# A two-layer trunk in split fp32 on one core: other PSUM banks for the short TensorE work, other steps for the seven-product form

## The chip, the cores and the metric

The kernel runs on one core of one Trainium2 chip. The metric is the device time of one execution in microseconds (us). The kernel before took 1900.27 us, the median of three runs (1898.66 to 1901.03). The trace was taken from a further execution, which took 1902.93 us as a whole, while the program's own instructions spanned 1900.6 us of it.

## The reference

The input is 256 tokens of 2048 numbers. Two layers follow one another, each a token mixer and a dense FFN, with an RMS norm ahead of each and a residual add behind it; a last norm ends it. The mixer of layer 0 is a causal pooling, that of layer 1 an attention with eight heads, each the difference of two softmaxes.

```python
def pool_mixer(h, w_grp, scale):            # layer 0; windows 2, 4, 8, 16
    ...
    pooled = jnp.stack([causal_trailing_mean(hg[:, :, g], POOL_WINDOWS[g]) for g in range(N_POOL_GROUPS)], axis=2)
    y = jnp.einsum('bsgc,gcd->bsgd', pooled - hg, w_grp)
    return y.reshape(B, S, D) * scale

def diff_attention(h, w_qkv, ...):          # layer 1
    qkv = h @ w_qkv
    ...
        s = jnp.where((dist >= 0)[None, None, None], s + bias[None, :, None], -jnp.inf)
        p = jax.nn.softmax(s, axis=-1)
        a = p[:, :, 0] - lam * p[:, :, 1]
        return jnp.einsum('bhqk,bkhe->bqhe', a.astype(v.dtype), v)
    ...
    o = rmsnorm(o, subln_g) * (1.0 - lambda_init)
    return o.reshape(B, S, H * e) @ w_o

def swiglu(h, wg, wu, wd):                  # wg, wu: 2048 x 5632, wd: 5632 x 2048
    return (jax.nn.silu(h @ wg) * (h @ wu)) @ wd
```

## The kernel before, in words

**One step of a group.** All large products go through `group` (line 139). A group gives a block of 256 tokens by 1024 columns as four blocks of 128 by 512, one for each half of the tokens and half of the columns. It adds up *steps*; each step takes 256 rows of the contraction, that is one activation tile (`xp`, `xq`, `h` or `oT`) and one weight load of 1 MB (`raw`, line 110). Every fp32 operand is split in a high and a low half: of the weights ScalarE writes the high half (`whi`, line 116) and VectorE the low one (`wlo`, line 117). A product of blocks is then three matmuls (high by high, high by low, low by high).

**Two forms of step.** A *plain* step makes the eight block products of a 2 by 2 multiplication: 24 matmuls. A *seven-product* step makes seven products of sums of blocks: 21 matmuls. For it VectorE adds the weight blocks (`tsum`, lines 122 to 125), ScalarE and VectorE split the sums (`thi` line 131, `tlo` line 132), and the activation tile is stored as eight sums of its blocks (the long branch of `pair`, lines 247 to 255). `tsum`, `thi` and `tlo` have one buffer each, `raw`, `whi` and `wlo` three. Which steps of a group are seven-product is written in the constants of lines 38 to 41.

**Banks.** The eight PSUM banks have fixed roles (line 136). The seven products go to banks 0 to 6 (M1 is 0, M6 1, M7 2, P5 3, P3 4, P4 5, M2 6). A plain step's four sums go to banks 6, 4, 5 and 7, three of which it shares with the seven products M2, P3, P4. So banks 0 to 3 are touched by seven-product steps alone. At the end of a group `combined` (line 182) makes the four blocks from the banks with two ScalarE copies (lines 188, 192) and eight VectorE operations (lines 189 to 198) into four SBUF tiles; a group of plain steps alone needs none of it, and returns the banks themselves.

**Short work.** Transposes (line 237 in `pair`, 441, 488), scores (456), the products with v (505 to 507) and the pooling products (311, 313) take a bank from `aux` (line 80), which goes round through banks 5, 6 and 7. A bank is a tile with one buffer: a later user in program order waits until the earlier one is read out. The pooling stage's sums take banks 0 to 4 through `acc`.

**Order.** The program lists, group by group, the steps, the combination and then the short work on the result. A scheduler of the framework lays down each engine's order when the kernel is built: of what its own reckoning has ready, it takes what comes first in the program, so that TensorE may go on with steps of the next group among short work of this one, unless banks or data forbid it.

**Stages.** Pooling mixer (lines 264 to 345), FFN of layer 0, attention, FFN of layer 1. An FFN goes in three chunks of 4, 4 and 3 groups of gate and up (eight steps each; scaled and multiplied at lines 368 and 369, transposed into `h`), and each chunk is followed by two groups of down (eight steps, six in the last chunk), which are added to the residual `x_tok` (line 387). In the last chunk of layer 0 the new residual is also transposed at once into the operand of the attention (line 396). Attention has four groups for q and k (line 478; scaled at 481, then two heads each), two groups for v (line 498; scaled at 501, then four heads each, which end in `oT`, line 517) and two for the output projection (line 520). The kernel ends with the last norm: squares (line 218), the row factor (lines 222, 207 to 212, 224), the scaling of the output tiles (lines 404 and 406) and four stores (line 407), two from SyncE's queue and two from ScalarE's.

Of the kernel before, what the change touches and what calls it, by code (L numbers as in the profile page):

```python
# [9 lines left out]
F32 = mybir.dt.float32  # L10
# [17 lines left out]

PLAIN = 2
WINDOWS = (2, 4, 8, 16)  # L30
LAMBDA_INIT = 0.8 - 0.6 * math.exp(-0.3)
QK_SCALE = 128.0 ** -0.5
MASKED = 1.0e30
# [1 line left out]
CHUNKS = (4, 4, 3)  # L35


SEVEN = (1, 4, 6)
SEVEN_DOWN = (1, 4)
SEVEN_QKV = (1, 4)  # L40
SEVEN_O = ()


B12, B11, B22, B21 = range(4)
# [6 lines left out]
def trunk_kernel(ctx, tc, x_n, gains, scale_in, final_in, subln, lam_in, band, dist,  # L51
# [21 lines left out]
    def bank(i, shape=(P, 512)):  # L73
        return psum.tile(list(shape), F32, name=f"b{i}", tag=f"b{i}")

    def acc(shape=(P, 512)):
        turn["acc"] += 1
        return bank(turn["acc"] % 5, shape)

    def aux(shape=(P, 512)):  # L80
        turn["aux"] += 1
        return bank(5 + turn["aux"] % 3, shape)


    gain_sb = const.tile([P, 6, NK], F32, name="gain_sb")
# [180 lines left out]
    with tc.tile_pool(name="start", bufs=1, reuse_waits="tile") as st:  # L266

        warm = tmp.tile([P, 8], F32, name="warm", bufs=1)
        nc.scalar.activation(warm[:, 0:1], ones[:, 0:1], AF.Sqrt)
        wp = aux()  # L270
        for _ in range(WARM):
            nc.tensor.matmul(wp[:, 0:P], ones, ones, start=True, stop=True)

        band_sb = st.tile([P, 4, 3, P], F32, name="band_sb")
        for t in range(2):
            for i in range(2):
                cols = slice(i * 1024, (i + 1) * 1024)
                nc.sync.dma_start(out=x_tok[:, t, cols], in_=x_n[:, t, cols])
        nc.scalar.dma_start(out=band_sb, in_=band)
        nc.scalar.dma_start(out=gain_sb, in_=gains)  # L280
        w_plain = [st.tile([P, 4, 512], F32, name=f"w{g}") for g in range(PLAIN)]
        for g in range(PLAIN):
            nc.sync.dma_start(out=w_plain[g], in_=pool_w[g])

        for t in range(2):
            ss_in = tmp.tile([P, 2, 4], F32, name="ss")
            sq = st.tile([P, 1024], F32, name="sq_in", bufs=2)
            for i in range(2):
                nc.scalar.activation(sq, x_tok[:, t, i * 1024:(i + 1) * 1024], AF.Square, accum_out=ss_in[:, 0, i:i + 1])
            tot = tmp.tile([P, 2], F32, name="ss_tot")  # L290
            nc.vector.tensor_tensor(tot[:, 0:1], ss_in[:, 0, 0:1], ss_in[:, 0, 1:2], ALU.add)
            r = rsqrt(tot[:, 0:1], D, 1)
            part = band_sb[:, :, 0:2] if t == 0 else band_sb[:, :, 2:3]
            nc.vector.tensor_scalar(part, part, r, None, ALU.mult)
        scale_sb = st.tile([P, D], F32, name="scale_sb")
        nc.scalar.dma_start(out=scale_sb, in_=scale_in)
        nc.scalar.dma_start(out=dist_sb, in_=dist)
        zp = [None] * 4

        def group_product(g):  # L300

            zp[g] = [acc() for _ in range(2)]
            if g < PLAIN:
                w = w_plain[g]
            else:
                hi, lo = halves(load(pool_w[g]))
            for i in range(2):
                ps = aux((P, 2, S))
                for k in range(2):
                    cols = slice((4 * g + 2 * i + k) * P, (4 * g + 2 * i + k + 1) * P)  # L310
                    nc.tensor.matmul(ps[:, k], x_tok[:, 0, cols], band_sb[:, g, 0:2].rearrange("p b s -> p (b s)"),  # L311
                                     start=True, stop=False)
                    nc.tensor.matmul(ps[:, k, P:], x_tok[:, 1, cols], band_sb[:, g, 2], start=False, stop=True)
                for k in range(2):
                    at = 2 * i + k
                    gain = gain_sb[:, 0, 4 * g + at:4 * g + at + 1]
                    if g < PLAIN:
                        a = st.tile([P, S], F32, name="mean", bufs=4)
                        nc.scalar.activation(a, ps[:, k], AF.Copy, scale=gain)
                        for t in range(2):  # L320
                            nc.tensor.matmul(zp[g][t], a[:, t * P:(t + 1) * P], w[:, at], start=(at == 0), stop=(at == 3))  # L321
                        continue
                    a = st.tile([P, 2, S], F32R, name="mean_hl", bufs=4)
                    split(a, ps[:, k], gain)
                    for t in range(2):
                        ah, al = (a[:, j, t * P:(t + 1) * P] for j in range(2))
                        for j, (u, y) in enumerate(((ah, hi), (ah, lo), (al, hi))):
                            nc.tensor.matmul(zp[g][t], u, y[:, at], start=(at == 0 and j == 0), stop=(at == 3 and j == 2))  # L328

        def residual(g):  # L330
            cols = slice(g * 512, (g + 1) * 512)
            for t in range(2):
                y = st.tile([P, 512], F32, name="y", bufs=2)
                nc.vector.tensor_tensor(y, zp[g][t], scale_sb[:, cols], ALU.mult)
                nc.vector.tensor_tensor(x_tok[:, t, cols], y, x_tok[:, t, cols], ALU.add)
                square_sum(ss, t, g)
            transposed(xq, g, 2, SEVEN)

        group_product(0)
        group_product(1)  # L340
        residual(0)
        group_product(2)
        residual(1)
        group_product(3)
        residual(2)
        residual(3)

    def ffn(layer, xq, ss, next_op, next_gain):
# [3 lines left out]
        with tc.tile_pool(name=f"ffn{layer}", bufs=1, reuse_waits="tile") as hp:  # L352
            g0 = 0
            ys = []
            for c, n in enumerate(CHUNKS):
# [19 lines left out]
                for o in range(2):  # L375
                    if last and o == 1:
# [1 line left out]
                        pre = tmp.tile([P, 8], F32, name="warm", bufs=1)  # L378
                        nc.scalar.activation(pre[:, 0:1], x_tok[:, 0, 0:1], AF.Square)
                        nc.scalar.activation(pre[:, 0:1], pre[:, 0:1], AF.Sqrt)  # L380
                    cs = combined(group([(hp_tiles[i], i in SEVEN_DOWN, w_down[layer][o, 2 * g0 + i])
                                         for i in range(2 * n)], hp), hp)
                    for b in range(2):
                        j = 2 * o + b
# [8 lines left out]
                                nc.vector.tensor_tensor(ys[j][:, t], x_tok[:, t, cols],  # L393
                                                        final_sb[j // 2][:, j % 2 * 512:j % 2 * 512 + 512], ALU.mult)
                        if last and next_op is not None:
                            transposed(next_op, j, next_gain, SEVEN_QKV)
                g0 += n
            if next_op is None:

                r = row_scale(ss_next)  # L400
                for j in range(4):
                    for t in range(2):
                        if t:
                            nc.vector.tensor_scalar(ys[j][:, t], ys[j][:, t], r[:, t:t + 1], None, ALU.mult)
                        else:
                            nc.scalar.activation(ys[j][:, t], ys[j][:, t], AF.Copy, scale=r[:, t:t + 1])
                    (nc.scalar if j % 2 else nc.sync).dma_start(
                        out=out[:, j * 512:(j + 1) * 512].rearrange("(t p) n -> p t n", p=P), in_=ys[j])
        return ss_next

    xp = operand(SEVEN_QKV)
    ss = ffn(0, xq, ss, xp, 3)


    ss_next = tmp.tile([P, 2, 4], F32, name="ss")
    with tc.tile_pool(name="attn", bufs=1, reuse_waits="tile") as ap_, ExitStack() as heads:
        at = heads.enter_context(tc.tile_pool(name="attn_tmp", bufs=2, reuse_waits="tile"))
        small = ap_.tile([P, 64], F32, name="small")
        qs_col, subln_sb, lam_sb, lp, le, neg_lam, gs = (
# [10 lines left out]
        nc.vector.scalar_tensor_tensor(neg_lam, le[:, 1:2], -LAMBDA_INIT, le[:, 0:1], ALU.add, ALU.subtract)  # L430
        nc.vector.tensor_scalar(gs, subln_sb, 1.0 - LAMBDA_INIT, None, ALU.mult)
        aT = []

        def transpose_probs(h, probs):

# [39 lines left out]

        for g in range(4):

            cs = combined(group([(xp[p], p in SEVEN_QKV, w_qk[g, p]) for p in range(NP)], ap_), ap_)
            for t in range(2):
                for b, scale in enumerate((qs_col, r_col)):  # L480
                    nc.scalar.activation(cs[t][b], cs[t][b], AF.Copy, scale=scale[:, t:t + 1])
            for u in range(2):
                qk = at.tile([P, 2, 2, S], F32, name="qk", bufs=3)
                for b in range(2):
# [10 lines left out]

        oT = [None] * NP
        for g in range(2):
            cs = combined(group([(xp[p], p in SEVEN_QKV, w_v[g, p]) for p in range(NP)], ap_), ap_)
            for b in range(2):
                for t in range(2):  # L500
                    nc.scalar.activation(cs[t][b], cs[t][b], AF.Copy, scale=r_col[:, t:t + 1])
            for h in range(4 * g, 4 * g + 4):
                v = [cs[t][h % 4 // 2][:, h % 2 * E:(h % 2 + 1) * E] for t in range(2)]
                op = aux((P, 2, E))
# [8 lines left out]
                on = at.tile([P, 2, E], F32, name="o_n", bufs=1)  # L513
                for t in range(2):
                    nc.scalar.activation(on[:, t, :], op[:, t, :], AF.Copy, scale=ro[:, t:t + 1])
                oT[h] = op_.tile(pair_shape(h in SEVEN_O), F32R, name=f"oT{h}")
                pair(oT[h], lambda i, t: on[:, t, i * P:(i + 1) * P], [gs[:, i:i + 1] for i in range(2)], h in SEVEN_O)
        xq = operand(SEVEN)
        for g in range(2):
            cs = combined(group([(oT[p], p in SEVEN_O, w_o[g, p]) for p in range(NP)], ap_), ap_)  # L520
            for b in range(2):
                j = 2 * g + b
                cols = slice(j * 512, (j + 1) * 512)
# [89 lines left out]
```

## Time and profile before

| | |
|---|---|
| median of three runs | 1900.27 us |
| profiled execution: its time, its span | 1902.93 us, 1900.6 us |
| TensorE busy, matmuls | 1854.4 us, 8248 |
| VectorE busy | 1554.5 us |
| ScalarE busy | 1010.3 us |
| read from HBM | 353.29 MB |
| granted TensorE clock, mean | 0.993 |

Times in the trace count from the span's start. A row of the timeline shows start, duration, engine, line, operation, output and inputs, shape and count, and in brackets the idle time of the engine ahead of it with what ended that. Matmuls overlap: the recorded duration of one is longer than the distance to the next, so that the cost of a matmul in a stream is read from the distance of starts. An fp32 matmul that isn't split appears as two records. PEld is TensorE's load of its stationary operand. PEclk is the share of full speed that TensorE's clock was granted.

The stages as the trace shows them: the pooling mixer to about 62 us, the FFN of layer 0 to 764, q and k to about 975, v and the heads' outputs to about 1095, the output projection to about 1186, the FFN of layer 1 to the end.

### The profile page before, as it was taken

Reading aid. Unit: us, or ns where it says so; the run is one execution under the profiler, and the core shown is the slowest. Engines: PE = TensorE matmul, PEld = TensorE weight load, DVE = VectorE, ACT = ScalarE, POOL = GpSimd, SP = SyncE. Lnnn points to the kernel's source line nnn. Section 1 sums busy time; section 2 is a strip of 40 time slices with the busy share of each in tenths; the row PEclk is TensorE's granted clock in tenths of the full one; section 3 lists DMA queues with packets and bytes.
Section 4 is the critical chain, followed back from the end, with each engine's and each line's share of the span. In section 5 each row is a group of like instructions: output and inputs, shape, how many; then the busy total and the mean of one; then the engine's idle time right before and its main releaser. Section 6 shows DMA issues by size and latency. Waiting matters only on the chain.

```text
span 1900.6 us, 20799 instructions
## 1 busy us (share of the span) xinstructions
PE 1854.4 (98%) x8248; PEld 1510.3 (79%) x8248; DVE 1554.5 (82%) x1577; ACT 1010.3 (53%) x979; POOL 0.7 (0%) x6
## 2 busy tenths in 40 slices
PE   8999999999999999999999999999999999999996
PEld 5788888888888887777777788888888888888885
DVE  4798988889888898977786645888878989888887
ACT  5565554555545556555555544555544555445554
POOL 0000000000000000000000000000000000000000
PEclk9999999999999999999999999999999999999998
DMA  6455565555555555544443545555655555565552
GB/s 263 156 199 200 179 210 209 185 206 200 190 203 189 199 182 197 185 163 152 163 155 133 177 155 180 177 196 189 211 201 207 191 200 196 199 230 189 200 200 89
DMA packets 50720, 356.72 MB, mean 188 GB/s; under 512 B 5952, under 2 KB 6080, under 8 KB 8000
## 3 DMA queue, kind: packets, MB, share of 16 engines
q1 hardware_dynamic: 49216, 351.30, 53.2%
q10 hardware_dynamic: 1408, 4.11, 0.6%
q8 instruction: 64, 1.05, 0.2%
q14 instruction: 32, 0.26, 0.0%
HBM read 353.29 MB, written 2.10 MB: 187 GB/s over the span
## 4 chain that ended last, share of the span: by engine, by line
PE 90%; DVE 5%; ACT 2%; DMA 2%; issue 1%; SPq 0%; ACTq 0%; DVEq 0%
PE b L178 86%; PE b L237 2%; DVE wlo L117 1%; ACT whi L116 1%; DMA raw<-w_qk 1%; DMA raw<-pool_w 1%; PE b L328 1%; PE b L321 1%; DVE x_tok L387 0%; DMA x_tok<-x_n 0%; PE b L456 0%; ACT sq L218 0%; DVE s_sb L458 0%; PE b L311 0%; DVE xp L230 0%
## 5 line engine op out<-in xcount | busy, mean ns | idle before, releaser
L178 PE MATMUL b<-whi,xp 128*128 128x512 f32 x2844 | 916.4, 393 | 5.0 <-DVE oT L230 2.2
L116 ACT CAST whi<-raw 128x2048 fp32r<-128x2048 f32 (+1 forms) x330 | 587.3, 1786 | 616.6 <-PE b L178 465.1
L117 DVE TENSOR_TENSOR wlo<-raw,whi 128x2048 fp32r<-128x2048 f32 (+1 forms) x330 | 700.6, 2129 | 233.2 <-ACT whi L116 231.6
L178 PEld LDWEIGHTS b<-whi,xp 128*128 128x128 f32 x2844 | 534.2, 188 | 123.8 <-issue 5.0
L178 PE MATMUL b<-wlo,xp 128*128 128x512 f32 x1422 | 557.1, 392 | 1.2 <-DVE wlo L117 1.2
L178 PE MATMUL b<-whi,h 128*128 128x512 f32 x1168 | 370.3, 390 | 1.1 <-ACT e L250 1.1
L178 PEld LDWEIGHTS b<-wlo,xp 128*128 128x128 f32 x1422 | 268.0, 188 | 56.3 <-DVE wlo L117 1.9
L178 PEld LDWEIGHTS b<-whi,h 128*128 128x128 f32 x1168 | 218.7, 188 | 47.3 <-ACT e L250 2.1
L132 DVE TENSOR_TENSOR tlo<-tsum,thi 128x2048 fp32r<-128x2048 f32 x98 | 223.9, 2285 | 14.9 <-ACT thi L131 14.3
L178 PE MATMUL b<-wlo,h 128*128 128x512 f32 x584 | 227.5, 390 | 0.2 <-DVE wlo L117 0.2
L178 PE MATMUL b<-thi,xp 128*128 128x512 f32 x592 | 209.6, 394 | 0.0
L131 ACT CAST thi<-tsum 128x2048 fp32r<-128x2048 f32 x98 | 187.2, 1911 | 24.2 <-DVE tsum L125 24.1
L122 DVE TENSOR_TENSOR tsum<-raw 128x1024 f32<-128x1024 f32 x98 | 119.5, 1219 | 15.3 <-DMA raw<-w_down 7.2
L178 PEld LDWEIGHTS b<-thi,xp 128*128 128x128 f32 x592 | 110.6, 188 | 22.4 <-ACT thi L131 0.4
L178 PEld LDWEIGHTS b<-wlo,h 128*128 128x128 f32 x584 | 109.7, 188 | 23.3 <-DVE wlo L117 0.6
L178 PE MATMUL b<-tlo,xp 128*128 128x512 f32 x296 | 115.7, 391 | 0.0
L178 PE MATMUL b<-whi,oT 128*128 128x512 f32 x256 | 82.7, 401 | 2.2 <-DVE oT L230 2.2
L124 DVE TENSOR_TENSOR tsum<-tsum,raw 128x512 f32<-128x512 f32 x98 | 67.5, 689 | 2.4
L125 DVE TENSOR_TENSOR tsum<-tsum,raw 128x512 f32<-128x512 f32 x98 | 67.3, 687 | 2.0
L178 PE MATMUL b<-thi,h 128*128 128x512 f32 x192 | 67.9, 393 | 1.0 <-ACT thi L131 1.0
L178 PEld LDWEIGHTS b<-tlo,xp 128*128 128x128 f32 x296 | 55.6, 188 | 11.8 <-DVE tlo L132 0.6
L178 PEld LDWEIGHTS b<-whi,oT 128*128 128x128 f32 x256 | 49.1, 193 | 12.9 <-issue 2.7
(127 smaller groups left out, 1143.1 us busy)
## 6 DMA issues: line engine op xcount, KB each, us to landing
raw<-w_gu SPq DMA_DIRECT2D x176, 1024.0 KB, 4.8
raw<-w_down SPq DMA_DIRECT2D x88, 1024.0 KB, 4.9
raw<-w_qk SPq DMA_DIRECT2D x32, 1024.0 KB, 5.1
raw<-w_v SPq DMA_DIRECT2D x16, 1024.0 KB, 4.8
raw<-w_o SPq DMA_DIRECT2D x16, 1024.0 KB, 4.9
x_tok<-x_n SPq DMA_DIRECT2D x4, 512.0 KB, 7.2
w<-pool_w SPq DMA_DIRECT2D x2, 1024.0 KB, 12.0
raw<-pool_w SPq DMA_DIRECT2D x2, 1024.0 KB, 13.3
```

Of the source, the lines that this page charges most:

```text
L116: nc.scalar.copy(hi[:, lo_block:], raw[:, lo_block:])
L117: nc.vector.tensor_tensor(lo[:, lo_block:], raw[:, lo_block:], f32(hi[:, lo_block:]), ALU.subtract)
L122: nc.vector.tensor_tensor(t[:, T1:T3 + 1], raw[:, B11:B22 + 1], raw[:, B12:B12 + 1].broadcast_to([P, 2, 512]), ALU.add)
L124: nc.vector.tensor_tensor(t[:, T2], t[:, T1], raw[:, B22], ALU.add)
L125: nc.vector.tensor_tensor(t[:, T4], t[:, T2], raw[:, B21], ALU.add)
L131: nc.scalar.copy(hi, t)
L132: nc.vector.tensor_tensor(lo, t, f32(hi), ALU.subtract)
L178: nc.tensor.matmul(ps[b], x, y[:, block], start=first, stop=(left[b] == 0))
L237: nc.tensor.transpose(ps[:, i, 1 - t if seven else t], src(i, t), ident)
L321: nc.tensor.matmul(zp[g][t], a[:, t * P:(t + 1) * P], w[:, at], start=(at == 0), stop=(at == 3))
L328: nc.tensor.matmul(zp[g][t], u, y[:, at], start=(at == 0 and j == 0), stop=(at == 3 and j == 2))
```

## The change

`aux` goes round through banks 0 to 3, `acc` through banks 4 to 7. The seven-product steps of gate and up move from 1, 4, 6 to 2, 4, 6 (the first group of each layer keeps 6 alone), those of down from 1, 4 to 2, 5, those of q and k from 1, 4 to 4, 6. v has plain steps alone, which are scaled from the banks into SBUF tiles of their own; the very last group of down has plain steps alone too. The sums of q and k get a pool of their own. The scaling of q and k goes column half by column half. In the pooling product the second block of the band, which is zero outside 16 columns, is a matmul of 16 columns of its own in place of the right half of a 256-column one. Of the last scaling, ScalarE keeps two of eight pieces in place of four.

```diff
+HALO = 16
-SEVEN = (1, 4, 6)
-SEVEN_DOWN = (1, 4)
-SEVEN_QKV = (1, 4)
-SEVEN_O = ()
+SEVEN = (2, 4, 6)
+SEVEN_DOWN = (2, 5)
+SEVEN_QK = (4, 6)
...
     def acc(shape=(P, 512)):
         turn["acc"] += 1
-        return bank(turn["acc"] % 5, shape)
+        return bank(4 + turn["acc"] % 4, shape)
 
     def aux(shape=(P, 512)):
         turn["aux"] += 1
-        return bank(5 + turn["aux"] % 3, shape)
+        return bank(turn["aux"] % 4, shape)
...
-                    nc.tensor.matmul(ps[:, k], x_tok[:, 0, cols], band_sb[:, g, 0:2].rearrange("p b s -> p (b s)"),
-                                     start=True, stop=False)
-                    nc.tensor.matmul(ps[:, k, P:], x_tok[:, 1, cols], band_sb[:, g, 2], start=False, stop=True)
+                    nc.tensor.matmul(ps[:, k, 0:P], x_tok[:, 0, cols], band_sb[:, g, 0], start=True, stop=True)
+                    nc.tensor.matmul(ps[:, k, P:], x_tok[:, 1, cols], band_sb[:, g, 2], start=True, stop=False)
+                    nc.tensor.matmul(ps[:, k, P:P + HALO], x_tok[:, 0, cols], band_sb[:, g, 1, 0:HALO], start=False, stop=True)
...
-                    cs = combined(group([(hp_tiles[i], i in SEVEN_DOWN, w_down[layer][o, 2 * g0 + i])
+                    by_seven = () if last and o and next_op is None else SEVEN_DOWN
+                    cs = combined(group([(hp_tiles[i], i in by_seven, w_down[layer][o, 2 * g0 + i])
                                          for i in range(2 * n)], hp), hp)
...
-                            transposed(next_op, j, next_gain, SEVEN_QKV)
+                            transposed(next_op, j, next_gain, SEVEN_QK)
...
-                        if t:
+                        if t or j > 1:
                             nc.vector.tensor_scalar(ys[j][:, t], ys[j][:, t], r[:, t:t + 1], None, ALU.mult)
...
+        hq = heads.enter_context(tc.tile_pool(name="qk_sums", bufs=1, reuse_waits="tile"))
...
+        def scaled(cs, scales, pool=None):
+            out = [[pool.tile([P, 512], F32, name="tok", tag=f"tok{t}{b}", bufs=2) if pool else cs[t][b] for b in range(2)]
+                   for t in range(2)]
+            for b, scale in enumerate(scales):
+                for t in range(2):
+                    nc.scalar.activation(out[t][b], cs[t][b], AF.Copy, scale=scale[:, t:t + 1])
+            return out
...
-            cs = combined(group([(xp[p], p in SEVEN_QKV, w_qk[g, p]) for p in range(NP)], ap_), ap_)
-            for t in range(2):
-                for b, scale in enumerate((qs_col, r_col)):
-                    nc.scalar.activation(cs[t][b], cs[t][b], AF.Copy, scale=scale[:, t:t + 1])
+            cs = combined(group([(xp[p], p in SEVEN_QK, w_qk[g, p]) for p in range(NP)], hq), hq)
+            cs = scaled(cs, (qs_col, r_col))
...
-            cs = combined(group([(xp[p], p in SEVEN_QKV, w_v[g, p]) for p in range(NP)], ap_), ap_)
-            for b in range(2):
-                for t in range(2):
-                    nc.scalar.activation(cs[t][b], cs[t][b], AF.Copy, scale=r_col[:, t:t + 1])
+            cs = scaled(combined(group([(xp[p], False, w_v[g, p]) for p in range(NP)], op_), op_), (r_col, r_col), op_)
```

More of the change, by code (lines that the diff above doesn't have):

```diff
@@ L409, in ffn @@
         return ss_next
-    xp = operand(SEVEN_QKV)
+    xp = operand(SEVEN_QK)
     ss = ffn(0, xq, ss, xp, 3)
@@ L515, in trunk_kernel @@
                     nc.scalar.activation(on[:, t, :], op[:, t, :], AF.Copy, scale=ro[:, t:t + 1])
-                oT[h] = op_.tile(pair_shape(h in SEVEN_O), F32R, name=f"oT{h}")
-                pair(oT[h], lambda i, t: on[:, t, i * P:(i + 1) * P], [gs[:, i:i + 1] for i in range(2)], h in SEVEN_O)
+                oT[h] = op_.tile(pair_shape(False), F32R, name=f"oT{h}")
+                pair(oT[h], lambda i, t: on[:, t, i * P:(i + 1) * P], [gs[:, i:i + 1] for i in range(2)], False)
         xq = operand(SEVEN)
         for g in range(2):
-            cs = combined(group([(oT[p], p in SEVEN_O, w_o[g, p]) for p in range(NP)], ap_), ap_)
+            cs = combined(group([(oT[p], False, w_o[g, p]) for p in range(NP)], ap_), ap_)
             for b in range(2):
```

## The prediction

> **What bounds the kernel now.** I read the page's busy times first, then the timeline of TensorE inside an FFN group, then the windows, one for each kind of group, and last the waits of TensorE.
>
> ```profile
> PE 1854.4 (98%) x8248; PEld 1510.3 (79%) x8248; DVE 1554.5 (82%) x1577; ACT 1010.3 (53%) x979; POOL 0.7 (0%) x6
> ```
>
> TensorE is busy for 98% of the span, but busy isn't at its peak: a matmul that waits behind its predecessor or runs at a lower clock counts as busy. So I need the price of a matmul in an undisturbed stream.
>
> ```profile
> 600.42 0.39 PE L178 MATMUL b<-wlo,xp 128*128 128x512 f32 x1
> 600.64 0.62 PE L178 MATMUL b<-whi,xp 128*128 128x512 f32 x2
> 601.10 0.39 PE L178 MATMUL b<-wlo,xp 128*128 128x512 f32 x1
> ```
>
> Three starts in 0.68 us: 0.2267 us for one matmul of line 178. A plain step is 24 of them (5.44 us), a seven-product step 21 (4.76 us). The pooling stage gives the short ones:
>
> ```profile
> 26.56 0.59 PE L311 MATMUL b<-band_sb,x_tok 128*128 128x256 f32 x2
> 26.99 0.38 PE L313 MATMUL b<-band_sb,x_tok 128*128 128x128 f32 x2
> 27.21 0.60 PE L311 MATMUL b<-band_sb,x_tok 128*128 128x256 f32 x2
> ```
>
> A record of 256 columns takes 0.215 us to the next start (0.43 for two), one of 128 columns 0.11, and a transpose has that last shape. Now the windows: one in the FFN, then one from the first scaling of a q and k group (809.43) to that of three groups later, one from the first scaling of the first v group to that of the second, one from there to the first read of the output projection's sums (1132.10); the last two rows split a stall of this stage from what follows it. Columns: length, busy time and records of PE, PEld, DVE, ACT and POOL, granted clock, DMA share, GB/s.
>
> ```profile
> 142.00:184.00 42.00, 42.00 (x191) 34.79 (x190) 37.12 (x33) 22.48 (x17) 0.00 (x0) 1.00 0.57 195
> 809.43:964.73 155.30, 149.06 (x669) 118.25 (x668) 120.28 (x188) 85.83 (x122) 0.00 (x0) 0.98 0.46 161
> 1015.59:1072.68 57.09, 52.39 (x228) 42.05 (x227) 32.78 (x49) 32.53 (x52) 0.00 (x0) 0.97 0.42 147
> 1072.68:1132.10 59.42, 54.49 (x230) 43.31 (x229) 26.91 (x39) 28.32 (x48) 0.00 (x0) 0.94 0.40 136
> 1086.00:1092.20 6.20, 3.68 (x16) 2.27 (x15) 2.44 (x11) 3.96 (x15) 0.00 (x0) 1.00 0.00 0
> 1092.20:1099.00 6.80, 5.79 (x16) 4.58 (x17) 1.76 (x6) 2.12 (x5) 0.00 (x0) 0.50 0.00 0
> ```
>
> In the FFN TensorE is never idle, so there is nothing to win there but matmuls. In attention there is.
>
> - A q and k group has 186 matmuls (42.2 us), 22 transposes and eight short score records (30 x 0.11 = 3.3) and eight of 256 columns (1.7): 47.2 us. The window gives 155.30 / 3 = 51.8. Lost: 4.6 us a group, 18.4 in four.
> - A v group has 186 matmuls (42.2), 24 records of 256 columns (5.2) and 16 transposes (1.8): 49.2 of 57.09, lost 7.9. The second v group's heads run under the output projection, with 192 matmuls (43.5): 50.5 of 59.42, lost 8.9. Together 16.8.
>
> So 35 of the 1900 us are lost in attention. Who held TensorE:
>
> ```profile
> PE b L178 <- DVE oT L230: 4.4, 2, 2.2
> PE b L237 <- ACT o_n L515: 3.7, 5, 1.0
> PE b L456 <- ACT aT L443: 2.5, 4, 0.6
> PE b L456 <- ACT qk L490: 2.0, 4, 0.7
> PE b L178 <- DVE xp L230: 1.9, 3, 1.0
> PE b L456 <- DVE s_sb L458: 1.5, 4, 0.4
> ```
>
> The first row is the telling one. Matmuls of line 178 do not read `oT` of the head just made; they waited 2.2 us twice for VectorE to read it out of its bank:
>
> ```profile
> 1093.21 0.76 PE L178 MATMUL b<-whi,oT 128*128 128x512 f32 x1 [2.22 <-DVE oT L230]
> ```
>
> This is a plain step of the output projection on early heads. Its data had been there, its bank (5, 6 or 7) had not: `aux` had lent it to the heads. Behind it, TensorE being in order, stood everything else. The scores' waits for `aT` and `s_sb` are waits for a lent bank too; those for `o_n` and `qk` are for data.
>
> **The change part by part.**
>
> *Banks 0 to 3 for the short work.* Plain steps touch banks 4 to 7 alone, so the next group's steps up to its first seven-product one can run whatever the heads are doing. In q and k that is now step 4: 4 x 5.44 = 21.8 us of free matmuls, against heads whose short work ran from its first transpose to its last for 18 us:
>
> ```profile
> 811.43 0.27 PE L488 MATMUL b<-ident,c 128*128 128x128 f32 x1
> ```
> ```profile
> 829.30 0.34 PE L441 MATMUL b<-ident,a_sb 128*128 128x128 f32 x1
> ```
>
> And VectorE then also had a seven-product step 1 to make, which it no longer has there. In v and the output projection no step needs banks 0 to 3 at all. So the bank waits go, and with them the low clock that followed them. What is late next is data: a transpose that the scheduler placed a little ahead of the ScalarE or VectorE result it takes. The two rows of that kind above sum to 5.7 us over all heads; I keep 0.95 us a q and k group and 1.5 us for each four output heads, 6.8 in all. Gain: 18.4 - 3.8 = 14.6 in q and k, 16.8 - 3.0 = 13.8 in v and output. Bounds: 35 (no residual) to 17 (half the loss stays as waits for data).
>
> The clock is part of that gain. In the 6.20 us up to 1092.2 TensorE was busy for 3.68, and in the 6.80 us that follow it was granted 0.50, which cost 3.4 us. By the Trainium skill, TensorE: Matmul & The Clock Gate, section "HAM oscillation", the clock falls back after a gap of over some 3.4 us without TensorE work; the trace disagrees, since the longest wait in the rows above is 2.2 us. By that rule the low clock would have another cause and stay, and the sum would be smaller by the second rival's price.
>
> *v plain.* Four seven-product steps become plain: 12 matmuls, 12 x 0.2267 = +2.7 us, all of it on TensorE's path. What goes is the VectorE work of those steps and the combination, which lay under matmuls.
>
> *Seven-product steps moved.* Same count in the FFN and in q and k, so no matmul is added; the cover is that VectorE has idle time (37.12 of 42 us busy). Price if the cover is gone: see the second rival. In the six-step groups of the last chunks, the last step is now a seven-product one, so that the combination starts late: five VectorE operations behind the last products, 5 x 0.68 = 3.4 us, hold banks 4, 5 and 7 for up to 3 us into the next group. The next plain step reaches its last bank only after 18 matmuls (4.1 us), so I expect under 1 us each time, at three places. Against it stand the waits for `xp` above (1.9 us, at the seam of layer 0's FFN and attention, largely for lent banks), which go. Net -1, bounds -2 and +3.
>
> *Band of 16 columns.* Sixteen times, two records of 256 columns become two of 128 and two of 16 with a load of the stationary operand each. Two records of 2 columns bound the new ones from below:
>
> ```profile
> 774.98 0.28 PE L428 MATMUL b<-small,ones 128*128 128x2 f32 x2
> 775.12 0.48 PE L178 MATMUL b<-whi,xp 128*128 128x512 f32 x1
> ```
>
> The pair took 0.14 us between long matmuls; from above stands 0.22, a pair of 128 columns. Before: 0.43 + 0.22 = 0.65. After: 0.22 + 0.22 + (0.14 to 0.22) = 0.58 to 0.66. I take 0.64, near the upper end, since here short records follow short ones: 16 x -0.01, about -0.2 us (bounds -1.1 and +0.2). Counted by columns alone, 112 columns fewer at 0.00084 us, 32 times, it would be -3.0. A rule speaks against that: by the Trainium skill, TensorE: Matmul & The Clock Gate, section "LDWEIGHTS", loading 128 columns takes about 107 ns however few columns then stream, which would make the saving nil. The 0.14 us for two records of 2 columns agrees with a floor of that kind.
>
> *The tail.* The last group plain: two steps more at 24, 6 x 0.2267 = +1.4 us, and no combination.
>
> ```profile
> 1886.11 0.39 PE L178 MATMUL b<-whi,h 128*128 128x512 f32 x1
> ```
> ```profile
> 1886.83 0.68 DVE L198 TENSOR_TENSOR c<-b,c 128x512 f32<-128x512 f32 x1
> 1887.43 1.28 DVE L387 TENSOR_TENSOR x_tok<-c,x_tok 128x512 f32<-128x512 f32 x2
> ...
> 1889.71 0.63 ACT L218 ACTIVATE sq<-x_tok 128x512 f32<-128x512 f32 x1
> 1890.25 0.19 ACT L218 ACTIVATION_READ_ACCUMULATOR sq<-x_tok 128x1 f32 x1
> 1890.47 0.16 DVE L222 TENSOR_REDUCE ss_tot<-ss 128x2 f32<-128x8 f32 x1 [0.55 <-ACT sq L218]
> ...
> 1892.09 1.95 ACT L406 ACTIVATE y<-y,r_tok 128x512 f32<-128x512 f32 x3 [1.02 <-DVE r_tok L224]
> 1892.09 1.67 DVE L404 TENSOR_SCALAR y<-y,r_tok 128x512 f32<-128x512 f32 x4
> ...
> 1894.68 0.40 ACTq L407 DMA_DIRECT2D out_t<-y  x1
> ```
>
> From TensorE's end (1886.11 + 0.39 = 1886.5) to the sum of squares (1890.47) it takes 4.0 us: the last combination, two adds, three squares in a row. With plain sums the four blocks come 6 matmuls (1.36 us) apart, so only the last add (0.64) and one square with its read (0.82) follow the end, with 0.3 for the first hand-over: 1.8. Gain 2.2. The scaling is a wash: six VectorE pieces at 1.67 / 4 = 0.42 are 2.5 us, ScalarE's chain took 2.6. The last group also loses the VectorE work of its two seven-product steps, and with it TensorE's idle time there, 36.00 - 35.34 = 0.7 us:
>
> ```profile
> 1850.00:1886.00 36.00, 35.34 (x156) 28.93 (x155) 32.91 (x37) 16.90 (x21) 0.00 (x0) 1.00 0.24 86
> ```
>
> Net 1.4 - 2.2 - 0.7 = -1.5 (bounds -3 and 0).
>
> *Sum.* -14.6 - 13.8 + 2.7 - 1 - 0.2 - 1.5 = -28.4, with the FFN at nought. Of the profiled execution's 1902.93 us, 2.3 lie outside its span, and it was 2.7 us above the median; the sum is a difference, so I take it off the median: 1900.27 - 28.4 = 1872.
>
> **The rivals.** A measurement of this kernel can tell about 0.2%, 3.8 us, from no change.
>
> *The waits turn into waits for data.* A head is a chain of some ten short operations, and if the scheduler places its transposes too early, TensorE stands there instead. If half the 35 us stay, 17.5 in place of the 6.8 kept: 1872 + 11 = 1883. For it: `o_n` waits up to 1.0. Against: FFN groups carry transposes behind ScalarE and VectorE work too, and lose nothing. Were all of it to come back in that way, the change would not do what it says: 1872 + 28 = 1900, no change; little speaks for it.
>
> *The low clock stays.* The granted clocks of 0.98, 0.97 and 0.94 in the three windows are 0.02 x 155 + 0.03 x 57 + 0.06 x 59 = 8.4 us of lost clock. If that comes by itself, 8.4 of the gain stay away: 1880. Against: the stretch shown lies right behind a stall, and the FFN window has 1.00. This is the rule of the Trainium skill from above, taken as a mechanism.
>
> *Slower: VectorE late in every gate and up group.* With 2, 4, 6 a seven-product step twice follows another with one plain step between; with 1, 4, 6 it did so once. `thi` and `tlo` have one buffer, so they can be written only between the last product of one and the third product of the next: a plain step and six matmuls, 5.44 + 1.36 = 6.8 us.
>
> ```profile
> 1872.85 2.29 DVE L117 TENSOR_TENSOR wlo<-raw,whi 128x2048 fp32r<-128x2048 f32 x1 [0.67 <-ACT whi L116]
> 1875.06 2.28 DVE L132 TENSOR_TENSOR tlo<-tsum,thi 128x2048 fp32r<-128x2048 f32 x1
> ```
> ```profile
> L131 ACT CAST thi<-tsum 128x2048 fp32r<-128x2048 f32 x98 | 187.2, 1911 | 24.2 <-DVE tsum L125 24.1
> ```
>
> In it go 1.91, then a `wlo` in service (2.29), then 2.28: 6.5. From 0.3 us more on, TensorE waits. Were `tlo` late by one further VectorE operation of 2.29 us at the new place in each of 20 groups (22 less the first of each layer), it would cost 20 x 2.0 = 40 us: 1872 + 40 = 1912. Against: the pair 4 and 6 stands now in the same groups, and the FFN window shows no idle time.
>
> **How the numbers follow.** Bank waits go, 1863 to 1878: 0.72. Half stays as data waits: 0.12. The clock stays: 0.07. No change: 0.04. VectorE late: 0.05. The range runs from 1863 (no residual in attention, tail and band at their good ends) to 1885, which takes in the half and the clock and leaves out about 0.2 with the tails. Faster by over 0.2%: 0.91; within: 0.04; slower: 0.05.
>
> **What would show it.** In the profile after: a q and k group in about 48 us, a v group in about 52; no row of TensorE's waits in which line 178 waits for `oT` or `s_sb`; granted clock 1.00 through attention; 18 more matmuls of line 178; the pooling products at 0.65 us a piece as before; about 1.8 us from TensorE's last matmul to the sum of squares. I would be wrong if FFN windows of 42 us show TensorE idle, or line 237 waits for `o_n` by several us a head.

## The result and the profile after

The kernel after takes 1865.72 us (median of six runs, 1865.41 to 1867.03), the kernel before on the same chip 1900.59. The ratio is 0.9821 with the interval 0.9809 to 0.9834, which is 34.9 us less. The forecast was 1872, with a range of 1863 to 1885. The profiled execution took 1866.35 us with a span of 1864.6; before's were 1902.93 and 1900.6. In the new kernel the lines have moved: the matmuls of a group are now line 180, the transposes of `pair` 239, the combination 190 to 200, the add to the residual 391, the squares 220, the last scaling 408 and 410.

First the busy times of the page:

```profile
PE 1840.9 (99%) x8298; PEld 1511.5 (81%) x8298; DVE 1509.8 (81%) x1531; ACT 1002.0 (54%) x965; POOL 0.7 (0%) x6
```

50 more records of TensorE and yet 13.5 us less busy time: what went was not work but matmuls that stood behind others or ran at half clock. The next rows are windows of the kernel after, cut by the same rule as those of before: one in the FFN, then from the first scaling of a q and k group to that of three groups later, from the first v group to the second, and from there to the first read of the output projection's sums.

```profile
141.30:184.00 42.70, 42.70 (x192) 35.00 (x191) 38.84 (x36) 24.17 (x19) 0.00 (x0) 1.00 0.58 197
803.78:947.18 143.40, 143.40 (x674) 116.90 (x673) 116.83 (x187) 86.68 (x121) 0.00 (x0) 1.00 0.52 176
996.09:1047.12 51.03, 51.03 (x233) 41.77 (x232) 24.07 (x36) 29.34 (x50) 0.00 (x0) 1.00 0.48 165
1047.12:1098.00 50.88, 50.87 (x231) 41.36 (x230) 24.28 (x36) 27.66 (x49) 0.00 (x0) 1.00 0.48 162
```

In attention busy time now equals the length and the clock column says 1.00. A q and k group takes 143.40 / 3 = 47.8 us, against 51.8 before and 47.2 by the count of its matmuls; the two windows of v fell from 57.09 and 59.42 to 51.03 and 50.88. The complete list of TensorE's waits (total us, times, longest) is short:

```profile
PE b L313 <- DVE band_sb L296: 6.3, 1, 6.3
PE b L180 <- DVE c L192: 3.1, 3, 1.0
PE b L274 <- DVE ones L91: 1.0, 1, 1.0
PE b L180 <- DVE c L197: 0.8, 2, 0.5
PE b L180 <- DVE wlo L119: 0.5, 1, 0.5
```

The waits for `oT`, `o_n`, `aT`, `qk`, `s_sb` and `xp` are gone. The first and third row belong to the start. The second is new, and the fourth (its line was 195) was 0.2 us before; they are taken up below.

To see where the 36.0 us between the two spans went, I counted the matmuls of `group` in each trace and took the recorded end of each group's last one. The right column is the first experiment, the new banks alone.

| from group's end to group's end | before, us | after | by change | new banks alone |
|---|---|---|---|---|
| start to first gate and up group | 101.4 | 99.0 | -2.3 | -2.1 |
| to the last gate and up group of layer 0 | 594.3 | 593.9 | -0.5 | -1.3 |
| two six-step groups of down, layer 0 | 68.6 | 67.6 | -1.0 | -3.0 |
| q, k and first v group | 254.6 | 239.2 | -15.4 | -17.8 |
| second v, first output group | 117.3 | 102.4 | -14.9 | -15.8 |
| to the first six-step group of down, layer 1 | 718.1 | 716.1 | -1.9 | -2.9 |
| last group | 32.3 | 34.6 | +2.3 | -0.7 |
| after TensorE's last matmul | 14.1 | 11.8 | -2.2 | 0.0 |

The first row is the least certain one: three kernels below that start as the kernel after does (the variants of the six-step groups, of v and of the last group) end it at 98.9, 98.3 and 98.2 us in their traces, so that differences of under 1 us in it tell nothing.

### The profile page after: what moved, and what is told of

It is laid out like the page before. It is cut to its first block, busy times and chain, and to the rows that moved or that the text cites. A ratio compares the mean times of both kernels' runs of the same rounds, so it can differ in the third digit from the quotient of the medians.

```text
span 1864.6 us, 20847 instructions
## 1 busy us (share of the span) xinstructions
PE 1840.9 (99%) x8298; PEld 1511.5 (81%) x8298; DVE 1509.8 (81%) x1531; ACT 1002.0 (54%) x965; POOL 0.7 (0%) x6
## 4 chain that ended last, share of the span: by engine, by line
PE 96%; DVE 1%; issue 1%; ACT 1%; DMA 0%; SPq 0%; DVEq 0%; ACTq 0%
PE b L180 91%; PE b L239 2%; PE b L323 1%; PE b L330 1%; PE b L470 1%; DMA x_tok<-x_n 0%; PE b L500 0%; ACT whi L118 0%; PE b L314 0%; PE b L313 0%; DVE wlo L119 0%; PE b L514 0%; PE b L516 0%; PE b L515 0%; PE b L455 0%
## 5 line engine op out<-in xcount | busy, mean ns | idle before, releaser
L119 DVE TENSOR_TENSOR wlo<-raw,whi 128x1536 fp32r<-128x1536 f32 (+1 forms) x330 | 706.0, 2139 | 285.2 <-ACT whi L118 285.0
L118 ACT CAST whi<-raw 128x1536 fp32r<-128x1536 f32 (+1 forms) x330 | 591.9, 1794 | 636.7 <-PE b L180 534.8
L180 PE MATMUL b<-whi,xp 128*128 128x512 f32 x2884 | 926.6, 392 | 1.0 <-DVE c L192 1.0
L180 PE MATMUL b<-whi,h 128*128 128x512 f32 x1188 | 377.0, 391 | 2.8 <-DVE c L192 2.1
L134 DVE TENSOR_TENSOR tlo<-tsum,thi 128x2048 fp32r<-128x2048 f32 x92 | 210.3, 2285 | 7.9 <-ACT thi L133 7.7
L180 PE MATMUL b<-thi,xp 128*128 128x512 f32 x560 | 195.2, 389 | 0.0
L133 ACT CAST thi<-tsum 128x2048 fp32r<-128x2048 f32 x92 | 175.6, 1909 | 13.7 <-DVE tsum L127 13.6
L124 DVE TENSOR_TENSOR tsum<-raw 128x1024 f32<-128x1024 f32 x92 | 112.3, 1220 | 2.5 <-DMA raw<-w_down 1.1
L127 DVE TENSOR_TENSOR tsum<-tsum,raw 128x512 f32<-128x512 f32 x92 | 63.3, 689 | 2.0
L126 DVE TENSOR_TENSOR tsum<-tsum,raw 128x512 f32<-128x512 f32 x92 | 63.1, 686 | 0.8
L180 PE MATMUL b<-thi,h 128*128 128x512 f32 x176 | 61.3, 389 | 0.0
```

Source lines behind the costliest of these rows:

```text
L118: nc.scalar.copy(hi[:, lo_block:], raw[:, lo_block:])
L119: nc.vector.tensor_tensor(lo[:, lo_block:], raw[:, lo_block:], f32(hi[:, lo_block:]), ALU.subtract)
L124: nc.vector.tensor_tensor(t[:, T1:T3 + 1], raw[:, B11:B22 + 1], raw[:, B12:B12 + 1].broadcast_to([P, 2, 512]), ALU.add)
L126: nc.vector.tensor_tensor(t[:, T2], t[:, T1], raw[:, B22], ALU.add)
L127: nc.vector.tensor_tensor(t[:, T4], t[:, T2], raw[:, B21], ALU.add)
L133: nc.scalar.copy(hi, t)
```

## The experiments

**The theories.** *Banks*: the gain comes from lending banks 0 to 3 in place of 5 to 7, and the steps were moved to keep seven-product steps out of the lent banks' way. *VectorE*: the gain comes from the relief of VectorE, which has no seven-product step 1 to make while the heads run, and none at all in v. Three kernels tell these apart or measure the banks, four measure single terms, and one puts the best together. Times are medians; each ratio is to the kernel before on the same chip. Two chips were used. On that of three banks, the six-step groups, v and the best of it, the kernel before took 1901.58 us, on that of the other four 1900.58 us, and beside the kernel after 1900.59 us. A difference between times from both chips is therefore uncertain by about 1 us.

**New banks alone.** The kernel before, with two lines changed:

```diff
-        return bank(turn["acc"] % 5, shape)
+        return bank(4 + turn["acc"] % 4, shape)
...
-        return bank(5 + turn["aux"] % 3, shape)
+        return bank(turn["aux"] % 4, shape)
```

> The kernel before with one edit: short work in banks 0 to 3, the pooling sums in 4 to 7; the seven-product steps stay where they were (1 and 4 in q, k and v). Bank theory: the short work then collides with the seven-product step 1, so that behind a q and k or v group only step 0 and the nine products of step 1 in banks 4 to 6 are free, 5.4 + 2.0 us against 18 us of heads; these seams keep most of their loss, and only the output projection, which has plain steps alone, loses its 8.8 us: about 1889 us (1885 to 1895). Rival, VectorE theory (the heads are slow because VectorE makes seven-product steps beside them, and the banks hardly matter): no gain but the pooling stage's 2, about 1898.

Measured: 1858.99 us, ratio 0.9782 (0.9768 to 0.9795), 41.6 less than before and 6.7 less than the whole change. Neither theory expected that. The windows, cut as above (q and k, first v, second v):

```profile
800.62:943.73 143.11, 143.11 (x672) 116.56 (x671) 120.87 (x188) 86.05 (x122) 0.00 (x0) 1.00 0.50 174
991.34:1041.17 49.83, 49.83 (x228) 40.63 (x227) 32.38 (x49) 31.82 (x52) 0.00 (x0) 1.00 0.49 169
1041.17:1092.07 50.90, 50.66 (x230) 41.08 (x229) 26.55 (x39) 27.55 (x48) 0.00 (x0) 1.00 0.48 159
```

VectorE (third pair of numbers behind the length) did 120.87 us of work over three groups, as before's 120.28, in 12 us less time, and TensorE was never idle. So VectorE's load was not what held TensorE; that theory falls. But my reason for moving the steps falls as well: I had a seven-product step 1 collide with the heads in banks 0 to 3. The timeline of TensorE shows what came of it (start, duration, engine, line):

```profile
814.08 0.39 PE L178 MATMUL b<-whi,xp 128*128 128x512 f32 x1
814.30 0.44 PE L441 MATMUL b<-ident,a_sb 128*128 128x128 f32 x2
814.50 0.47 PE L178 MATMUL b<-thi,xp 128*128 128x512 f32 x1
814.81 0.39 PE L178 MATMUL b<-tlo,xp 128*128 128x512 f32 x1
815.04 0.40 PE L178 MATMUL b<-thi,xp 128*128 128x512 f32 x1
...
817.92 0.39 PE L178 MATMUL b<-thi,xp 128*128 128x512 f32 x1
```

The group began at 803.0, and its first product with `thi`, the high half of step 1's sums, stands at 814.50. The windows of line 178 alone, up to there and on to the end of the heads' short work, count what TensorE did of the group meanwhile (length, busy time and records of PE and PEld, clock, DMA share, GB/s):

```profile
803.00:814.50 11.50, 8.55 (x32) 5.30 (x31) 1.00 0.50 182
814.50:823.80 9.30, 9.20 (x38) 6.88 (x38) 1.00 0.39 126
```

Two of the first window's 32 records only reach into it: the last matmul of the group before (802.77) and the `thi` one itself. The other 30 are as many as the 24 of step 0 and the six of M1 and M2, which are step 1's own and need no sums. Between the first product with `thi` and the second (817.92) stand ten more matmuls on `whi` and `wlo`. Step 1 has only nine of that kind in all (M1, M2 and P3), so that of these 40 at least seven come from a step other than 0 and 1. TensorE thus had matmuls for the time of the heads, and in these windows of q and k it was never idle. The trace doesn't number the banks: that the order was laid down so that each product found its bank free is inferred.

The pool of their own for the sums of q and k and the new order of their scaling weren't timed alone; without them, here, q and k are as fast as in the kernel after.

**The rest of the change with the old banks.** The kernel after, with those two lines put back.

> The changed kernel with the short work back in banks 5 to 7 and the pooling sums in 0 to 4; plain v, moved seven-product steps, 16-column band and the plain last group stay. Bank theory: the first steps of every group are now plain and want just the banks that are lent, and the products of step 1 in banks 0 to 3, which filled the time before, are gone, so the seams in attention lose as much as before or more, and FFN seams begin to lose too, half a us to 2 us each at 44 seams: 1915 us (1900 to 1970), slower than the kernel before. VectorE theory: heads beside plain steps are quick, most of the gain stays: about 1872.

Measured: 1966.39 us, ratio 1.0348 (1.0333 to 1.0362), 66 slower than before and in the range of the bank theory, above its likeliest value. Against the kernel after it loses 4 us up to the first gate and up group, 26 in the rest of layer 0's FFN, 52 in attention and 18 in layer 1's FFN. The first three rows of TensorE's waits and one further down, then a stall in the FFN: a window up to it and one behind it.

```profile
PE b L180 <- DVE c L197: 23.6, 16, 6.2
PE b L180 <- ACT whi L118: 7.6, 6, 1.6
PE b L313 <- DVE band_sb L296: 6.7, 1, 6.7
...
PE b L180 <- DVE tlo L134: 2.0, 4, 1.3
```
```profile
185.60:192.40 6.80, 4.91 (x21) 3.45 (x19) 6.80 (x9) 2.69 (x3) 0.00 (x0) 1.00 0.77 289
192.40:199.30 6.90, 5.08 (x13) 4.01 (x14) 5.95 (x8) 2.53 (x2) 0.00 (x0) 0.51 0.00 1
```

16 times the next group's plain steps waited for VectorE to read the last sums of the group before. In the first window VectorE is busy for all of 6.80 us. VectorE late in the gate and up groups was my third rival, and with the old banks it does come, but not where I had put it: the rival had TensorE wait for `tlo`, which makes 2.0 us here, while the seams make 23.6. Why VectorE's order puts the combination so late with these banks and steps wasn't settled.

The two kernels make a square: old banks with old steps 1900.6, new banks with old steps 1859.0, old banks with new steps 1966.4, both new 1865.7. The banks are worth 42 or 101 us, the rest costs 66 or 7.

**Three lent banks instead of four.** As the first kernel, but `aux` goes round through banks 0 to 2, so that the number of lent banks is as before and only their place is new.

> As the run with the banks alone, but the short work goes round through three banks, 0 to 2, as many as before. If it matters which banks the short work has: about as fast as with four, 1859 to 1862. If it matters that there is one more: most of the gain goes, 1880 to 1900.

Measured: 1864.06 us, ratio 0.9807 (0.9790 to 0.9823). That is 5.1 us above four banks, just over the first range; against the kernel before on each one's own chip it is 37.5 us of gain in place of 41.6. So nearly all of the gain comes from which banks are lent, and 4 to 5 us from the fourth one.

**The six-step groups with a plain last step.** The kernel after with seven-product steps 2 and 4 in place of 2 and 5 in the down groups of the last chunks (and two tags of `h` changed over, so that the tiles fit).

```diff
+SEVEN_SHORT = (2, 4)
...
+                seven_down = SEVEN_SHORT if last else SEVEN_DOWN
...
-                    by_seven = () if last and o and next_op is None else SEVEN_DOWN
+                    by_seven = () if last and o and next_op is None else seven_down
```

> The changed kernel with seven-product steps 2 and 4 in place of 2 and 5 in the six-step groups of down (the last group stays plain), so that these groups too end on a plain step. If the late combination behind a seven-product last step costs what the stalls in the changed trace add up to (1.2 + 0.6, 1.2 + 0.6 and 1.2 + 0.4 us at three places): -5, 1861. If it costs only what the prediction allowed (three times under 1 us): -1 to -3, 1863 to 1865. If those stalls have another cause: 1866.

Measured: 1860.95 us, ratio 0.9788 (0.9773 to 0.9802), 4.8 less than the kernel after, as the first case of the expectation has it; by the spans of the two traces it is 5.8 (1858.8 against 1864.6). What it removes is seen in the kernel after, first on TensorE, then on VectorE:

```profile
724.75 0.39 PE L180 MATMUL b<-thi,h 128*128 128x512 f32 x1
726.17 0.47 PE L180 MATMUL b<-whi,h 128*128 128x512 f32 x1 [1.04 <-DVE c L192]
...
729.89 0.40 PE L180 MATMUL b<-whi,h 128*128 128x512 f32 x1
730.75 0.50 PE L180 MATMUL b<-whi,h 128*128 128x512 f32 x1 [0.47 <-DVE c L197]
```
```profile
722.41 2.29 DVE L119 TENSOR_TENSOR wlo<-raw,whi 128x2048 fp32r<-128x2048 f32 x1
724.62 0.68 DVE L191 TENSOR_TENSOR c<-b,c 128x512 f32<-128x512 f32 x1
725.34 0.69 DVE L192 TENSOR_TENSOR c<-b,c 128x512 f32<-128x512 f32 x1
```

The group's last product starts at 724.75. The next group's first plain product wants bank 6, which line 192 reads until 726.03. Starts are 1.42 and 0.86 us apart there in place of 0.23: 1.8 us lost at this seam, and in the same way 1.8 at 760 and, in the last group, 1.6 at 1818. In the experiment the whole list of TensorE's waits has two rows, both of the start:

```profile
PE b L314 <- DVE band_sb L297: 6.3, 1, 6.3
PE b L275 <- DVE ones L92: 1.1, 1, 1.1
```

**Seven-product steps in v.** The kernel after with steps 4 and 6 of v as seven-product steps; the sums are then in SBUF and are scaled there.

> The changed kernel with seven-product steps 4 and 6 in the two groups of v, whose results are scaled in place again. If the heads need nothing but banks apart, v's seven-product steps were no hindrance and plain steps cost their 12 matmuls: -2.7 us, 1863. If v had to be plain for the heads to run free of stalls: equal or slower, 1866 to 1875.

Measured: 1864.07 us, ratio 0.9805 (0.9790 to 0.9819), 1.65 less than the kernel after. The two v groups become 1.4 and 1.0 us shorter, where 6 matmuls make 1.36; the first output group becomes 0.5 longer, which leaves 1.9 by the traces. So v didn't have to be plain for the heads to run free of stalls.

**The band.** The kernel after with before's 256-column matmul in the pooling product.

> The changed kernel with the band's second block back in one matmul of 256 columns. The changed profile is 2.3 to 2.6 us ahead by the end of the first gate and up group. If the band made that: 2 us or more come back, 1868. If the records of 16 columns are worth 0.07 us a piece, as their distances in the changed profile say: 16 x 0.07 = 1.1, 1867. If the other banks of the pooling stage made it: nothing, 1865.7.

Measured: 1866.77 us (1866.72 to 1866.91), ratio 0.9822 (0.9809 to 0.9836): 1.05 more than the kernel after, whose own runs spread from 1865.41 to 1867.03. The spans of the two traces differ by 0.4 us (1865.0 and 1864.6). That 1.05 is sixteen times 0.066 looks like the second case, but the rows of the kernel after don't bear it out:

```profile
36.52 0.39 PE L313 MATMUL b<-band_sb,x_tok 128*128 128x128 f32 x2
36.74 0.39 PE L314 MATMUL b<-band_sb,x_tok 128*128 128x128 f32 x2
36.96 0.29 PE L315 MATMUL b<-band_sb,x_tok 128*128 128x16 f32 x2
37.10 0.47 PE L313 MATMUL b<-band_sb,x_tok 128*128 128x128 f32 x2
37.41 0.39 PE L314 MATMUL b<-band_sb,x_tok 128*128 128x128 f32 x2
37.63 0.29 PE L315 MATMUL b<-band_sb,x_tok 128*128 128x16 f32 x2
37.77 0.47 PE L313 MATMUL b<-band_sb,x_tok 128*128 128x128 f32 x2
```

The first piece takes 0.58 us (36.52 to 37.10), but the next one 0.67 (37.10 to 37.77), and so do those behind it: the pair of 16 columns makes way after 0.14, but the pair behind it then takes 0.31 in place of 0.22. The trace shows why: the loads of the stationary operand (PEld) start 0.112 us apart, two for each pair, that of 16 columns too, and six of them make 0.67. Before's piece, with four loads, took 0.65 (26.56 to 27.21). Four pieces in a row take 2.60 us in the kernel after (45.78 to 48.38) and 2.61 with the 256-column matmul (45.88 to 48.49). So the band is worth next to nothing in these rows, which are at full clock. What made the 1.05 isn't shown; in its trace TensorE waits 2.2 us for `mean` at the start, a row that the kernel after doesn't have.

**The last group.** The kernel after with seven-product steps 2 and 5 in the very last group too.

```diff
-                    by_seven = () if last and o and next_op is None else SEVEN_DOWN
+                    by_seven = SEVEN_DOWN
```

> The changed kernel with seven-product steps 2 and 5 in the very last group of down too. TensorE saves 6 x 0.227 = 1.4 us there; the combination comes back behind the last products and is late, as its last step is now a seven-product one. By the tail of the kernel before (4.0 us from TensorE's end to the sum of squares against 1.8 now) plus up to 1.5 for the late combination: +1 to +2.5 us, 1867 to 1868. If the combination hides after all: -1.4, 1864.3.

Measured: 1869.75 us, ratio 0.9839 (0.9826 to 0.9853), 4.0 more than the kernel after and beyond what I expected. Its last group is 1.5 us shorter, but from TensorE's end (1849.98 + 0.39) to the sum of squares it takes 7.5 us, since the combination comes behind the last product:

```profile
1849.98 0.39 PE L180 MATMUL b<-thi,h 128*128 128x512 f32 x1
...
1852.10 0.69 DVE L197 TENSOR_TENSOR c<-b,c 128x512 f32<-128x512 f32 x1
1852.70 0.68 DVE L198 TENSOR_TENSOR c<-b,c 128x512 f32<-128x512 f32 x1
1853.29 0.68 DVE L200 TENSOR_TENSOR c<-b,c 128x512 f32<-128x512 f32 x1
1853.89 1.29 DVE L391 TENSOR_TENSOR x_tok<-c,x_tok 128x512 f32<-128x512 f32 x2
...
1857.84 0.16 DVE L224 TENSOR_REDUCE ss_tot<-ss 128x2 f32<-128x8 f32 x1
```

**The best of it.** Before's steps with the new banks, the 16-column band, the plain last group and the new split of the last scaling.

> The kernel before with the short work in banks 0 to 3 and the pooling sums in 4 to 7, the band of 16 columns, the plain last group and six of the eight last scalings on VectorE; seven-product steps all where they were before, in v too. Sum of the parts so far: 1859.0 of the banks alone, -1.1 for the band, and for the last group +1.4 in matmuls and -2.2 in the tail: 1857 (1856 to 1858.5).

Measured: 1857.91 us (1857.46 to 1858.53), ratio 0.9772 (0.9757 to 0.9786): 1.1 less than the banks alone and 7.8 less than the kernel after, beside both of which the kernel before took 1.0 us less; by the spans of the traces it is 1.4 and 9.1. It is the fastest version of all.

## Why the prediction was right, and where its sizes were off

The mechanism was the one named: TensorE waited for lent banks. With the edit of the banks alone those waits are gone and 41.6 us with them. By stages, the forecast of -28.4 became -36.0 in the traces; the errors partly cancel.

- *Waits in attention.* Forecast -14.6 and -13.8, with +2.7 for v: -25.7. Measured -15.4 and -14.9 by the table: -30.3. The term that was mis-sized is the 6.8 us that I kept for waits for data: by this sum 2.2 were left (35.2 lost before, less 30.3 and 2.7). The rows of `o_n` and `qk` from which I took it followed from the lent banks: both are gone, no row of a head's data has taken their place, and with the edit of the banks alone just 0.2 us of `o_n` is left. The first rival (half stays, 1883) falls with it.
- *The clock.* It went as argued: 1.00 in every window of attention. The second rival falls, as the low clock came with the stalls: before has four stretches of half clock in attention, the kernel after and the banks alone none, and the old banks with the new steps have twelve between the first and the last group. Eleven of these twelve follow waits of at most 2.3 us, as the pair of windows above shows, and the first of before's (826.0) follows waits of at most 0.7 us. By the Trainium skill, TensorE: Matmul & The Clock Gate, section "HAM oscillation", it takes a gap of more than some 3.4 us. Only one stretch comes near that, which begins 2.8 us into the wait of 6.2; the others rather fit the page's section "A second HAM failure mode: psum-queue depth-cycling", by which frequent short idling between groups is enough.
- *Why the steps were moved.* "The next group's steps up to its first seven-product one can run whatever the heads are doing" is true, but it wasn't needed. With steps 1 and 4 the three q and k groups are as fast (143.11 against 143.40 us), since TensorE's order has other matmuls where I saw a collision.
- *Moved steps at the seams.* I wrote "under 1 us each time, at three places", counting from the bank that a plain step reaches last. The wait is at the first one, bank 6, to which I gave no price: line 192 reads it only at 725.34, behind a `wlo` of 2.29 us and line 191 on VectorE, although its product, M2, comes second of the step's seven in the program. It cost 1.6 to 1.8 us a seam in the trace and 1.6 (4.8 / 3) to 1.9 by the experiment. The gain against it, put at 1.9 for `xp`, was larger: the FFN rows of the table without the last group sum to -3.4 after and to -7.2 with the banks alone.
- *v plain.* +2.7 by count of matmuls; taken back in place it gave 1.65 by the medians and 1.9 by the traces, as the output group lost 0.5.
- *Band.* I took 0.64 us a piece, nearly the 0.65 of before, and so it is: 0.67 in a row, a little less where a block ends. But the bound from below, 0.14 for two records of 2 columns, was misread. It is the distance to the next start; the matmul there (775.12) then stands 0.31 from its successor in place of 0.23, so that this pair cost 0.22 too. By the Trainium skill, TensorE: Matmul & The Clock Gate, section "LDWEIGHTS", I had the saving as nil. The trace agrees with that rule: the loads stand 0.112 us apart where the rule has about 107 ns, whereas 0.14 for two of them would not have agreed. The start's -2.3 is then not the band's; with the banks alone it is -2.1, and what made it wasn't taken apart.
- *The tail.* From TensorE's end to the sum of squares I said 1.8 us in place of 4.0; the rows below give 1.7 (1852.35 + 0.39 to 1854.46), and the scaling ends as forecast, with six VectorE pieces in 2.46 us. But the last group began with the late combination of the group before, so that last group and tail together gave +0.1, not -1.5. With that combination early they give -1.8 (44.5 us against 46.3).

```profile
1852.35 0.39 PE L180 MATMUL b<-whi,h 128*128 128x512 f32 x1
...
1852.77 0.69 DVE L391 TENSOR_TENSOR x_tok<-b,x_tok 128x512 f32<-128x512 f32 x1
...
1853.71 0.63 ACT L220 ACTIVATE sq<-x_tok 128x512 f32<-128x512 f32 x1
...
1854.46 0.16 DVE L224 TENSOR_REDUCE ss_tot<-ss 128x2 f32<-128x8 f32 x1 [0.27 <-ACT sq L220]
...
1856.09 2.46 DVE L408 TENSOR_SCALAR y<-y,r_tok 128x512 f32<-128x512 f32 x6
```

- *VectorE late.* The third rival didn't come with the new banks: the FFN window has TensorE busy for 42.70 of 42.70 us. With the old ones VectorE was late, though at the seams and not at `tlo`; the same steps can be free or cost tens of microseconds, by which banks the short work holds.

Of the 6.7 us by which the whole change trails the banks alone, 4.8 (late combination) and 1.65 (v) are measured. The table's two rows of gate and up groups trail by 0.8 and 1.0 us as well, which no experiment took apart, and the plain last group takes some of it back.

## What to carry to other kernels

Lend short work the accumulators that the next long work touches last, and look for the waits of a long product on a read that has nothing to do with its data: that is a bank, and it costs all that is queued behind it. End a group on a step whose sums are combined while the next one runs, or the seam waits. Time each part of a change alone: here two lines gave more than the whole.

## What was unexpected in the hardware

A matmul of 16 columns cost as much as one of 128: the next start comes after 0.14 us a pair in place of 0.22, but the pair behind it pays that back, as the loads of the stationary operand come 0.112 us apart. And half clock followed clusters of waits none of which, but for one of 6.2 us, was longer than 2.3; once none was longer than 0.7. Each stretch of half clock between the first and the last group lasted 3.4 or 6.8 us.
